# Gate and up columns of a feed-forward network by seven block products, in chunks of eight feature tiles

## The chip, the cores and the metric

One core of a Trainium2 chip. The metric is the device time of one execution in microseconds (us). The engines are TensorE (PE; its weight loads are listed apart as PEld), VectorE (DVE), ScalarE (ACT), GpSimd (POOL) and SyncE (SP), which issues most transfers. POOL can issue transfers too. Each engine executes its own instructions in order and waits on semaphores for the others.

## The reference

Two layers. Each adds a feed-forward network, a mixer and a second feed-forward network to x (512 tokens of 1024 features):

```python
def _rms_norm(x, g):
    y = xf * lax.rsqrt(jnp.mean(xf * xf, axis=-1, keepdims=True) + NORM_EPS)
    return y.astype(x.dtype) * g

def _swiglu(x, w_gate, w_up, w_down):
    return (jax.nn.silu(x @ w_gate) * (x @ w_up)) @ w_down

for l in range(DEPTH):
    x = x + 0.5 * _swiglu(_rms_norm(x, norm_ffn1[l]), ffn1_w_gate[l], ffn1_w_up[l], ffn1_w_down[l])
    h = _rms_norm(x, norm_mix[l])
    ...
    x = x + mix @ w_out[l]
    x = x + 0.5 * _swiglu(_rms_norm(x, norm_ffn2[l]), ffn2_w_gate[l], ffn2_w_up[l], ffn2_w_down[l])
```

The hidden size is 2816, so w_gate and w_up have 22 columns of 128 features, called features f below, and w_down has 8 columns of 128. All is float32. The mixer (three head groups: a recurrence, windowed attention and a convolution) isn't touched, apart from where one scratch buffer lies.

## The kernel before

x is held transposed: eight tiles x[j] of 128 features by 512 tokens. Every matrix is split into two parts that TensorE takes at its full pace: hi, the value cast to the reduced format F32R, and lo, the rest. A product of 128 x 128 weights with a tile is then three matmuls (`mm3`, L116): hi with the high part of x (L119), hi with its low part (L120), lo with the high part (L121). A weight block (`slot`, L105) is loaded by SP (L111) into one of three raw buffers, cast to hi by ACT (L112), and lo is a DVE subtract (L113); hi and lo have three buffers each.

A feed-forward network (`ffn`) first computes, for each f, the gate column and the up column. Each is 8 tiles x 3 matmuls of 512 tokens into one PSUM bank, 48 matmuls for an f. `gated` then multiplies gate (L216, DVE) and up (L218, DVE) by R, the norm's factor for each token, applies Silu (L217, ACT), multiplies both (L219, POOL), and splits the result into ah (L124, ACT) and al (L125, DVE), which stay in SBUF for all 22 features. Then each of the 8 down columns is one sum of 22 x 3 matmuls in PSUM, and L271 (DVE) adds half of it to x[j].

The norm is applied late: `norm_tile` gives xh (x times the norm's gain, cast, L172, ACT), xl (the rest, L173, DVE) and the square (L180, ACT), which POOL adds up (L181). The products run on xh and xl; the sum over features (L199, PE) and R follow while feature 0 and 1 are computed. At the mixer's end, x[j] gets its sum in L717 (DVE), and norm_tile(j) prepares the second network's input tile by tile. At the kernel's start the loads of the first two weight blocks stand among those of x.

The order of the work on each engine is set by a scheduler that looks at readiness, not by the order of the code alone. Tiles come from pools with a fixed number of buffers: a new tile waits for the last use of the one whose buffer it takes.

Of the kernel before, what the change touches and what calls it, by code (L numbers as in the profile page):

```python
# [21 lines left out]
EPS = 1e-6  # L22
RB = 3
# [15 lines left out]
HD = 64  # L39
NP = 3  # L40
# [41 lines left out]
class Kern:  # L82
# [71 lines left out]
    def tb(self, n):  # L154
        return self.tab[:, TAB[n][0] : TAB[n][1]]

    def norm_begin(self, idx):
        self.xp = self.tc.tile_pool(name=self.n("xp"), bufs=1, side="right")
        pool = self.xp.__enter__()
        xh = lambda j: pool.tile([P, T], F32R, tag=f"xh{j}", name=self.n("xh"))  # L160
        xl = lambda j: pool.tile([P, T], F32R, tag=f"xl{j}", name=self.n("xl"))
        self.xh, self.xl = [xh(j) for j in range(KT)], [xl(j) for j in range(KT)]
        pool.tile([P, XPAD], F32, name=self.n("xpad"))
        self.nidx = idx
        self.acc = self.nrm.tile([P, T], F32, tag="acc", name=self.n("acc"))

    def norm_tile(self, j):

        nc = self.nc
        x = self.x[j]  # L170
        g = self.gains[:, self.nidx * KT + j : self.nidx * KT + j + 1]
        nc.scalar.activation(self.xh[j], x, AF.Copy, scale=g)  # L172
        nc.vector.scalar_tensor_tensor(  # L173
            self.xl[j], x, g, self.xh[j].bitcast(F32), op0=ALU.mult, op1=ALU.subtract
        )
        if j == 0:
            nc.scalar.activation(self.acc, x, AF.Square)
        else:
            sq = self.nrm.tile([P, T], F32, tag=("sq", "R")[j % 2], name=self.n("sq"))
            nc.scalar.activation(sq, x, AF.Square)  # L180
            nc.gpsimd.tensor_tensor(self.acc, self.acc, sq, op=ALU.add)  # L181
# [31 lines left out]
    def gated(self, f, p, ap, tp, ah, al):
        nc = self.nc
        t = [tp.tile([P, T], F32, tag=q, name=self.n(q)) for q in ("g", "u", "s")]
        nc.vector.tensor_tensor(t[0], p[0], self.R, op=ALU.mult)  # L216
        nc.scalar.activation(t[2], t[0], AF.Silu)  # L217
        nc.vector.tensor_tensor(t[1], p[1], self.R, op=ALU.mult)  # L218
        nc.gpsimd.tensor_tensor(t[2], t[2], t[1], op=ALU.mult)  # L219
        ah.append(ap.tile([P, T], F32R, name=self.n("ah")))  # L220
        al.append(ap.tile([P, T], F32R, name=self.n("al")))
        self.split(ah[f], al[f], t[2])

    def ffn(self, l, n, nxt, last=False):
        nc, I = self.nc, self.I
        with self.tc.tile_pool(name=self.n("ffn"), bufs=1) as ap, self.tc.tile_pool(name=self.n("fft"), bufs=2) as tp:
            ah, al = [], []
            held = None
            for f in range(FT):
                p = []  # L230
                if f == 0 and l == 0 and n == 0:

                    both = [self.ahead.pop(0) for w in range(2)]
                    p = [self.psum() for w in range(2)]
                    for k in range(KT):
                        for (hi, lo), ps in zip(both, p):
                            s = slice(k * P, (k + 1) * P)
                            self.mm3(ps, hi[:, s], lo[:, s], self.xh[k], self.xl[k], k == 0, k == KT - 1)
                    self.norm_sum()
                    held = p  # L240
                    continue
                for w in range(2):
                    hi, lo = self.ahead.pop(0) if self.ahead else self.slot(I["wgu"][l, n, f, w], 1024)
                    ps = self.psum()
                    for k in range(KT):
                        s = slice(k * P, (k + 1) * P)
                        self.mm3(ps, hi[:, s], lo[:, s], self.xh[k], self.xl[k], k == 0, k == KT - 1)
                    p.append(ps)
                    if (f, w) == (0, 1):
                        self.norm_sum()  # L250
                    elif (f, w) == (1, 0):
                        self.norm_spread()
                if f == 0:
                    held = p
                    continue
                if held:
                    self.gated(f - 1, held, ap, tp, ah, al)
                    held = None
                self.gated(f, p, ap, tp, ah, al)
            self.norm_close()  # L260
            if nxt is not None:
                self.norm_begin(nxt)
            for j in range(KT):
                ps = self.psum()
                for q in range(0, FT, 8):
                    m = min(8, FT - q)
                    hi, lo = self.slot(I["wd"][l, n, j, :, q * P : (q + m) * P], m * P)
                    for k in range(m):
                        s = slice(k * P, (k + 1) * P)
                        self.mm3(ps, hi[:, s], lo[:, s], ah[q + k], al[q + k], q + k == 0, q + k == FT - 1)  # L270
                nc.vector.scalar_tensor_tensor(  # L271
                    self.x[j], ps, 0.5, self.x[j], op0=ALU.mult, op1=ALU.add
                )
                if nxt is not None:
                    self.norm_tile(j)
                    if nxt % 3 == 1:
                        nc.sync.dma_start(out=self.xs[:, j], in_=self.x[j])
                if last:
                    nc.sync.dma_start(out=self.out[:, j], in_=self.x[j])

    def feed(self, srcs):

# [7 lines left out]
    def mixer(self, l):  # L290
# [747 lines left out]
    def run(self):  # L1038
        nc, tc, I = self.nc, self.tc, self.I
        self.consts()  # L1040
        self.x = []
        for j in range(KT):
            if j in (0, 1):
                self.ahead.append(self.slot(I["wgu"][0, 0, 0, j], 1024))
            self.x.append(self.xt(j))
            nc.sync.dma_start(out=self.x[j], in_=I["xT"][:, j])
        self.xs = self.dp.tile([P, KT, T], F32, name="xs")
        self.norm_begin(0)
        for j in range(KT):
            self.norm_tile(j)  # L1050
        self.consts2()
        for l in range(self.depth):
            self.ffn(l, 0, 3 * l + 1)
            self.mixer(l)
# [24 lines left out]
def arrays(i):  # L1079
# [7 lines left out]
    A["wgu"] = c(gu.reshape(L, 2, 2, KT, P, FT, P).transpose(0, 1, 5, 2, 4, 3, 6).reshape(L, 2, FT, 2, P, KT * P))  # L1087
# [44 lines left out]
```

## Time and profile before

| | |
|---|---|
| median of 3 runs | 2079.12 us (2079.01 to 2082.44) |
| the profiled execution | 2079.0 us |
| its span, first to last instruction | 2077.2 us |
| ACT busy | 743.7 us (36%) |
| POOL busy | 335.5 us (16%) |
| read from HBM | 183.47 MB |

The span is shorter than the execution by 1.8 us, which lie around it. Busy times of PE are modelled at the end of a matmul, so what a matmul costs is read from the distance between starts. A group of instructions is a line with its engine, operation and tiles; its row gives the count, the busy time, the mean, and the idle time just before them with what ended it. A window's row gives for each engine the busy time in that stretch and the number of instructions, then the granted clock of TensorE as a share, the share of the transfer engines in use and GB/s.

### The profile page before, as it was taken

Reading aid. Unit: us, or ns where it says so; the run is one execution under the profiler, and the core shown is the slowest. Engines: PE = TensorE matmul, PEld = TensorE weight load, DVE = VectorE, ACT = ScalarE, POOL = GpSimd, SP = SyncE. Lnnn points to the kernel's source line nnn. Section 1 sums busy time; section 2 is a strip of 40 time slices with the busy share of each in tenths; the row PEclk is TensorE's granted clock in tenths of the full one; section 3 lists DMA queues with packets and bytes.
Section 4 is the critical chain, followed back from the end, with each engine's and each line's share of the span. In section 5 each row is a group of like instructions: output and inputs, shape, how many; then the busy total and the mean of one; then the engine's idle time right before and its main releaser. Section 6 shows DMA issues by size and latency. Waiting matters only on the chain. (4 is left out here: it accounts for less than half of the span.)

```text
span 2077.2 us, 26018 instructions
## 1 busy us (share of the span) xinstructions
PE 2033.1 (98%) x10406; PEld 1654.5 (80%) x10406; DVE 1122.4 (54%) x1565; ACT 743.7 (36%) x1136; POOL 335.5 (16%) x298
## 2 busy tenths in 40 slices
PE   8999999989999999999999999999899999999999
PEld 6888888768877788888888888887687677888887
DVE  5545433699766455543244554337997764454422
ACT  4332322454365332322232322325534653232221
POOL 3101101132411211110010111002323111110100
PEclk9999999999999999999999999999999999999999
DMA  4232333213212323233323232332133132333332
GB/s 169 92 102 93 95 109 124 80 57 92 78 42 89 109 92 99 94 97 100 98 91 102 92 101 89 120 112 90 44 92 90 33 105 92 94 100 102 99 109 66
DMA packets 81865, 193.80 MB, mean 93 GB/s; under 512 B 26640, under 2 KB 32272, under 8 KB 81744
## 3 DMA queue, kind: packets, MB, share of 16 engines
q1 hardware_dynamic: 81312, 191.79, 29.7%
q8 instruction: 81, 1.33, 0.3%
q10 hardware_dynamic: 432, 0.36, 0.1%
q14 instruction: 40, 0.33, 0.1%
HBM read 183.47 MB, written 8.65 MB: 92 GB/s over the span
## 5 line engine op out<-in xcount | busy, mean ns | idle before, releaser
L112 ACT CAST hi<-raw 128x1024 fp32r<-128x1024 f32 (+3 forms) x368 | 350.9, 954 | 991.0 <-PE psg L120 850.0
L113 DVE TENSOR_TENSOR lo<-raw,hi 128x1024 fp32r<-128x1024 f32 (+3 forms) x368 | 504.1, 1370 | 348.7 <-ACT hi L112 329.2
L119 PE MATMUL psg<-xh,hi 128*128 128x512 f32 x1632 | 642.9, 394 | 7.1 <-ACT xh L172 7.1
L120 PE MATMUL psg<-xl,hi 128*128 128x512 f32 x1632 | 641.1, 393 | 5.0 <-DVE xl L173 4.9
L121 PE MATMUL psg<-xh,lo 128*128 128x512 f32 x1632 | 641.0, 393 | 0.0
L120 PEld LDWEIGHTS psg<-xl,hi 128*128 128x128 f32 x1632 | 308.6, 189 | 74.3 <-DVE xl L173 8.9
L119 PEld LDWEIGHTS psg<-xh,hi 128*128 128x128 f32 x1632 | 308.6, 189 | 73.8 <-ACT xh L172 7.1
L121 PEld LDWEIGHTS psg<-xh,lo 128*128 128x128 f32 x1632 | 308.8, 189 | 66.4 <-issue 2.0
L119 PE MATMUL psg<-ah,hi 128*128 128x512 f32 x704 | 273.9, 389 | 0.0
L120 PE MATMUL psg<-al,hi 128*128 128x512 f32 x704 | 273.9, 389 | 0.0
L121 PE MATMUL psg<-ah,lo 128*128 128x512 f32 x704 | 273.9, 389 | 0.0
L219 POOL TENSOR_TENSOR s<-s,u 128x512 f32<-128x512 f32 x88 | 120.5, 1370 | 800.1 <-ACT hi L112 676.5
L218 DVE TENSOR_TENSOR u<-psg,R 128x512 f32<-128x512 f32 x88 | 60.8, 691 | 265.4 <-PE psg L121 265.1
L120 PEld LDWEIGHTS psg<-al,hi 128*128 128x128 f32 x704 | 132.2, 188 | 27.5
L121 PEld LDWEIGHTS psg<-ah,lo 128*128 128x128 f32 x704 | 132.2, 188 | 27.5
L119 PEld LDWEIGHTS psg<-ah,hi 128*128 128x128 f32 x704 | 132.2, 188 | 27.3
L216 DVE TENSOR_TENSOR g<-psg,R 128x512 f32<-128x512 f32 x88 | 60.8, 691 | 125.4 <-PE psg L121 125.4
L181 POOL TENSOR_TENSOR acc<-acc,sq 128x512 f32<-128x512 f32 x42 | 58.6, 1396 | 381.3 <-ACT sq L180 380.9
L1001 DVE SCALAR_TENSOR_TENSOR cacc<-z,par,cacc 128x482 f32<-128x482 f32 (+14 forms) x120 | 101.7, 847 | 1.7
L124 ACT CAST ah<-s 128x512 fp32r<-128x512 f32 x88 | 54.8, 623 | 121.7 <-POOL s L219 121.7
L125 DVE TENSOR_TENSOR al<-s,ah 128x512 fp32r<-128x512 f32 x88 | 59.8, 679 | 20.9 <-ACT ah L124 20.9
L867 PE MATMUL psg<-hi,xh 128*128 128x384 f32 x192 | 68.0, 357 | 1.3 <-ACT nat L892 1.3
(208 smaller groups left out, 1819.2 us busy)
## 6 DMA issues: line engine op xcount, KB each, us to landing
raw<-in_wgu_dram SPq DMA_DIRECT2D x176, 512.0 KB, 3.5
raw<-in_wd_dram SPq DMA_DIRECT2D x64, 512.0 KB, 3.5
raw<-in_win_dram SPq DMA_DIRECT2D x28, 512.0 KB, 3.5
raw<-in_wd_dram SPq DMA_DIRECT2D x32, 384.0 KB, 3.1
raw<-in_watt_dram SPq DMA_DIRECT2D x24, 384.0 KB, 3.0
raw<-in_wout_dram SPq DMA_DIRECT2D x28, 192.0 KB, 2.3
xs<-x SPq DMA_DIRECT2D x16, 256.0 KB, 2.0
x<-xs SPq DMA_DIRECT2D x16, 256.0 KB, 3.1
```

Of the source, the lines that this page charges most:

```text
L112: nc.scalar.copy(hi[:, :cols], raw[:, :cols])
L113: nc.vector.tensor_tensor(lo[:, :cols], raw[:, :cols], hi[:, :cols].bitcast(F32), op=ALU.subtract)
L119: mm(out, lhsT=whi, rhs=xhi, start=first, stop=False)
L120: mm(out, lhsT=whi, rhs=xlo, start=False, stop=False)
L121: mm(out, lhsT=wlo, rhs=xhi, start=False, stop=last)
L125: self.nc.vector.tensor_tensor(lo, src, hi.bitcast(F32), op=ALU.subtract)
L181: nc.gpsimd.tensor_tensor(self.acc, self.acc, sq, op=ALU.add)
L216: nc.vector.tensor_tensor(t[0], p[0], self.R, op=ALU.mult)
L218: nc.vector.tensor_tensor(t[1], p[1], self.R, op=ALU.mult)
L219: nc.gpsimd.tensor_tensor(t[2], t[2], t[1], op=ALU.mult)
L867: mm(o, lhsT=self.xh[kk][:, t], rhs=hi[:, s], start=kk == 0, stop=False)
L1001: nc.vector.scalar_tensor_tensor(a[:, d:], z[:, 0 : T - d], pa("dww", u * CW + j), a[:, d:], op0=ALU.mult, op1=ALU.add)
```

## The change

The tokens are cut into halves of 256, the eight x tiles into even and odd ones, and the gate and up columns are taken as the two halves of the output. That makes a 2 x 2 block product, which seven block products give instead of eight (Strassen's kind, with few additions). Each of the seven is 4 pairs of tiles x 3 matmuls of 256 tokens: 84 matmuls of 256 for an f, where there were 48 of 512.

For it the code adds:
- `norm_forms`: of every pair of x tiles seven forms (sums and differences of the halves), each split into fh (ACT) and fl (DVE). It takes the place of L172 and L173 for the two feed-forward networks; the mixer's norm keeps them.
- `forms`: the weights' seven forms of a feature. ba (two blocks) and s13 (two blocks) are loaded by SP; a transfer issued by POOL adds two further blocks onto s13 as it lands (L281). s24 is made by two DVE sums (L284, L285). dd, the seventh block, is loaded for two features at a time. The low parts of s13 and s24 are DVE subtracts (L269). Those of ba and dd are made by ACT writing -hi (L266) and a transfer issued by POOL that adds raw onto it (L267); in the first feature of the kernel they are subtracts too. s13 and s24 share three buffers, ba and dd the three raw ones.
- In `up`, one ACT copy and seven DVE adds of 256 (L334) put the four output blocks together; the scalings by R (L314, L316) then read SBUF.
- Chunks: after eight features (8, 8, 6) the eight down columns take them in, with a sum onto x each (L373), so there are three such rounds where there was one.
- The loads of the kernel's first weights are issued ahead of x's. The scratch of `norm_forms` for the second network lies in a buffer of the mixer.

The rows below are what DVE executes for one feature in the middle of the first network. Before (g and u are the scaled columns, lo a low part of weights, al of the result):

```order
L216 TENSOR_TENSOR g_688<-psg_632,R_279 128x512
L113 TENSOR_TENSOR lo_732<-raw_730,hi_731 128x1024
L218 TENSOR_TENSOR u_689<-psg_663,R_279 128x512
L113 TENSOR_TENSOR lo_774<-raw_772,hi_773 128x1024
L125 TENSOR_TENSOR al_696<-s_690,ah_695 128x512
```

And of the change, from the third add of one feature to its al:

```order
L334 TENSOR_TENSOR u_1863<-psb_1906,u_1863 128x256
L334 TENSOR_TENSOR u_1863<-psg_1878,u_1863 128x256
L269 TENSOR_TENSOR lo_1987<-s_314_1973,hi_1986 128x1024
L334 TENSOR_TENSOR g_1862<-psb_1921,g_1862 128x256
L334 TENSOR_TENSOR g_1862<-psg_1935,g_1862 128x256
L314 TENSOR_TENSOR g_1862<-g_1862,R_442 128x512
L284 TENSOR_TENSOR s_338_2113<-s_337_2110,ba_2108 128x512
L334 TENSOR_TENSOR u_1863<-psg_1949,u_1863 128x256
L269 TENSOR_TENSOR lo_1991<-s_316_1978,hi_1990 128x1024
L316 TENSOR_TENSOR u_1863<-u_1863,R_442 128x512
L285 TENSOR_TENSOR s_338_2113<-s_338_2113,ba_2108 128x512
L130 TENSOR_TENSOR al_1968<-g_1862,ah_1967 128x512
```

Two subtracts of 1024 are still there. Seven adds of L334 (two stand ahead of these rows) and the sums of the weights two features on (s_338 from s_337, which is an s13 with its second part already added) have come between them, ahead of al.

The second place is the start of the second feed-forward network of layer 0 on DVE. Before, from the sum onto the last x tile but one (psg of L717 is the mixer's output product):

```order
L717 TENSOR_TENSOR x_1049_5547<-psg_993_5350,x_1049_5547 128x512
L113 TENSOR_TENSOR lo_1064_5628<-raw_1062_5626,hi_1063_5627 128x1024
L717 TENSOR_TENSOR x_1054_5570<-psg_997_5372,x_1054_5570 128x512
L173 SCALAR_TENSOR_TENSOR xl_1016_5413<-x_1049_5547,gains_85,xh_1008_5405 128x512
L113 TENSOR_TENSOR lo_1069_5666<-raw_1067_5664,hi_1068_5665 128x1024
L173 SCALAR_TENSOR_TENSOR xl_1017_5414<-x_1054_5570,gains_85,xh_1009_5406 128x512
```

And of the change, from the sum onto the last tile (L848 is L717 of before; eo is the scratch, fl the low parts of forms):

```order
L848 TENSOR_TENSOR x_6995<-psg_6770,x_6995 128x512
L202 SCALAR_TENSOR_TENSOR fl_6803<-eo_6805,fh_6799 128x512
L192 TENSOR_TENSOR eo_6805<-eo_6805 128x256
L204 TENSOR_TENSOR fl_6803<-eo_6805,fh_6799 128x768
L194 SCALAR_TENSOR_TENSOR fl_6804<-eo_6805,fh_6800 128x256
L195 TENSOR_TENSOR fl_6804<-eo_6805,fh_6800 128x256
L198 TENSOR_TENSOR eo_6805<-eo_6805 128x256
L199 TENSOR_TENSOR eo_6805<-eo_6805 128x256
L200 TENSOR_TENSOR eo_6805<-eo_6805 128x256
L202 SCALAR_TENSOR_TENSOR fl_6804<-eo_6805,fh_6800 128x512
L227 TENSOR_SCALAR rnt<-psc_7179 128x4
L204 TENSOR_TENSOR fl_6804<-eo_6805,fh_6800 128x768
```

Where one low part of x stood behind the last sum, there are now the rest of two pairs of forms. Behind the last row come the two sums of s24 (L284, L285) and the two low parts (L269) of feature 0's weights. The load into that feature's s13 by SP waits for the form in the last row.

The third place is POOL in the same stretch as the first: transfers that add (DMA) and the products of `gated` (g times u) in one queue.

```order
L317 TENSOR_TENSOR g_1862<-g_1862,u_1863 128x512
L281 DMA s_357_2240<-in_wgu_dram 128x1024
L267 DMA lo_1995<-dd_1975 128x1024
L317 TENSOR_TENSOR g_1999<-g_1999,u_2000 128x512
L267 DMA lo_2115<-ba_2108 128x1024
L281 DMA s_380_2377<-in_wgu_dram 128x1024
```

Before, POOL had one product a feature here and no transfer; now two or three transfers are issued between two products.

The diff, cut to its core:

```diff
+    def norm_forms(self, j):
+        ...
+        if j % 2 == 0:
+            A.activation(e, x3, AF.Copy, scale=self.gains[:, g : g + 1])
+            A.activation(h[:, 0], e[:, 0], AF.Copy, scale=-1.0)
+            V.tensor_tensor(tf[:, 0], e[:, 1], e[:, 0], op=ALU.subtract)
+            A.copy(h[:, 3], tf[:, 0])
+            V.scalar_tensor_tensor(l[:, 0], e[:, 0], -1.0, f32(h[:, 0]), op0=ALU.mult, op1=ALU.subtract)
+            V.tensor_tensor(l[:, 3], tf[:, 0], f32(h[:, 3]), op=ALU.subtract)
+        else:
+            A.activation(o, x3, AF.Copy, scale=self.gains[:, g : g + 1])
+            V.tensor_tensor(tf[:, 1], o[:, 1], tf[:, 0], op=ALU.subtract)
+            V.tensor_tensor(tf[:, 2], e[:, 1], o[:, 1], op=ALU.subtract)
+            V.tensor_tensor(tf[:, 3], o[:, 0], tf[:, 1], op=ALU.subtract)
+            A.activation(h[:, 1:3], o, AF.Copy, scale=-1.0)
+            V.scalar_tensor_tensor(l[:, 1:3], o, -1.0, f32(h[:, 1:3]), op0=ALU.mult, op1=ALU.subtract)
+            A.copy(h[:, 4:7], tf[:, 1:4])
+            V.tensor_tensor(l[:, 4:7], tf[:, 1:4], f32(h[:, 4:7]), op=ALU.subtract)
+    def forms(self, l, n, f):
+        def parts(pool, tag, raw, dma):
+            ...
+            A.copy(hi, raw)
+            if dma:
+                A.activation(lo, hi.bitcast(F32), AF.Copy, scale=-1.0)
+                G.dma_start(out=lo, in_=raw, accum_op=ALU.add)
+            else:
+                V.tensor_tensor(lo, raw, hi.bitcast(F32), op=ALU.subtract)
+            return hi, lo
+        first = f == 0 and l == 0 and n == 0
+        ba = v(self.ring.tile([P, 1024], F32, tag="raw", name=self.n("ba")))
+        nc.sync.dma_start(out=ba, in_=v(w[l, n, f, :, 0 : 2 * k]))
+        s13 = self.ep.tile([P, 2, k], F32, tag="rs", name=self.n("s13"), bufs=ER)
+        nc.sync.dma_start(out=s13, in_=v(w[l, n, f, :, k : 3 * k]))
+        if f % 2 == 0:
+            dd = v(self.ring.tile([P, 1024], F32, tag="raw", name=self.n("dd")))
+            nc.sync.dma_start(out=dd, in_=w[l, n, f : f + 2, :, 3 * k : 4 * k].rearrange("f p k -> p f k"))
+        G.dma_start(out=s13, in_=v(w[l, n, f, :, 2 * k : 4 * k]), accum_op=ALU.add)
+        s24 = self.ep.tile([P, 2, k], F32, tag="rs", name=self.n("s24"), bufs=ER)
+        hba, lba = parts(self.ring, "i", ba, not first)
+        V.tensor_tensor(s24[:, 0], s13[:, 1], ba[:, 1], op=ALU.add)
+        V.tensor_tensor(s24[:, 1], s24[:, 0], ba[:, 0], op=ALU.add)
+        h13, l13 = parts(self.ep, "s", s13, False)
+        h24, l24 = parts(self.ep, "s", s24, False)
+        if f % 2 == 0:
+            self.hdd = parts(self.ring, "i", dd, not first)
+        ...
     def ffn(self, l, n, nxt, last=False):
+            def up(f, W, held):
+                def mul(i, r=range(KP)):
+                    ...
+                    for p in r:
+                        s = slice(p * P, (p + 1) * P)
+                        self.mm3(ps[i], hi[:, s], lo[:, s], self.fh[p][:, c], self.fl[p][:, c], p == 0, p == KP - 1)
+                add = lambda o, i, z: V.tensor_tensor(o, ps[i], z, op=ALU.add)
+                mul(1)
+                A.copy(g0, ps[1])
+                mul(5)
+                if f == 0:
+                    for i in (6, 7, 2, 3):
+                        mul(i, range(KP - 1))
+                    r = [KP - 1]
+                else:
+                    r = range(KP)
+                mul(6, r)
+                add(u1, 6, g0)
+                add(g1, 5, u1)
+                ...
+                mul(7, r)
+                add(u0, 7, u1)
+                add(u1, 5, u0)
+                mul(2, r)
+                add(g0, 2, g0)
+                mul(3, r)
+                add(g1, 3, g1)
+                mul(4)
+                add(u0, 4, u0)
+                ...
+            for q in range(0, FT, CH):
+                m = min(CH, FT - q)
+                items += [("up", f, q, m) for f in range(q, q + m)] + [("down", j, q, m) for j in range(KT)]
-        GG = [m1.tile([P, NC, 2, 2, HD], F32, name=self.n("GG")) for _ in range(NP)]
+        GG = [m1.tile([P, NC * 4 * HD], F32, tag=f"GG{q}", name=self.n("GG")).rearrange("p (c x h t) -> p c x h t", c=NC, x=2, h=2) for q in range(NP)]
-        self.norm_begin(3 * l + 2)
+        self.norm_begin(3 * l + 2, lambda: m1.tile([P, 8 * HT], F32, tag="GG0", name=self.n("eo")))
```

More of the change, by code (lines that the diff above doesn't have):

```diff
@@ L28 @@
 CPOS = 4
+HT = T // 2
+KP = KT // 2
+CH = 8
+ER = 3
+ES = 4
 CO = (1, 1)
@@ L165, in norm_begin @@
         self.acc = self.nrm.tile([P, T], F32, tag="acc", name=self.n("acc"))
+    def norm_forms(self, j):
+        nc = self.nc
+        V, A = nc.vector, nc.scalar
+        g = self.nidx * KT + j
+        e, o, tf = self.eo[:, 0], self.eo[:, 1], self.tf
+        h, l = self.fh[j // 2], self.fl[j // 2]
+        f32 = lambda a: a.bitcast(F32)
+        x3 = self.x[j].rearrange("p (t c) -> p t c", t=2)
+        if j % 2 == 0:
[14 more added lines that the diff above has]
+            V.tensor_tensor(l[:, 4:7], tf[:, 1:4], f32(h[:, 4:7]), op=ALU.subtract)
     def norm_tile(self, j):
@@ L170, in norm_tile @@
         x = self.x[j]
[L171 to L175, printed above, removed]
+        if self.nidx % 3 == 1:
+            g = self.gains[:, self.nidx * KT + j : self.nidx * KT + j + 1]
+            nc.scalar.activation(self.xh[j], x, AF.Copy, scale=g)
+            nc.vector.scalar_tensor_tensor(
+                self.xl[j], x, g, self.xh[j].bitcast(F32), op0=ALU.mult, op1=ALU.subtract
+            )
+        else:
+            self.norm_forms(j)
         if j == 0:
@@ L211, in norm_close @@
         self.xp.__exit__(None, None, None)
[L213 to L222, printed above, removed]
+    def forms(self, l, n, f):
+        nc, w = self.nc, self.I["wgu"]
+        V, A, G = nc.vector, nc.scalar, nc.gpsimd
+        k = KP * P
+        def parts(pool, tag, raw, dma):
+            hi = pool.tile([P, 2, k], F32R, tag="h" + tag, name=self.n("hi"), bufs=RB if tag == "i" else ES)
+            lo = pool.tile([P, 2, k], F32R, tag="lo" if tag == "i" else "ls", name=self.n("lo"), bufs=RB if tag == "i" else ES)
+            A.copy(hi, raw)
+            if dma:
+                A.activation(lo, hi.bitcast(F32), AF.Copy, scale=-1.0)
+                G.dma_start(out=lo, in_=raw, accum_op=ALU.add)
+            else:
+                V.tensor_tensor(lo, raw, hi.bitcast(F32), op=ALU.subtract)
+            return hi, lo
+        first = f == 0 and l == 0 and n == 0
+        v = lambda a: a.rearrange("p (x k) -> p x k", x=2)
+        ba = v(self.ring.tile([P, 1024], F32, tag="raw", name=self.n("ba")))
[14 more added lines that the diff above has]
+            self.hdd = parts(self.ring, "i", dd, not first)
+        hd, ld = self.hdd
+        return {
+            1: (hba[:, 1], lba[:, 1], 0),
+            2: (hba[:, 0], lba[:, 0], 1),
+            3: (h24[:, 1], l24[:, 1], 2),
+            4: (hd[:, f % 2], ld[:, f % 2], 6),
+            5: (h13[:, 1], l13[:, 1], 3),
+            6: (h24[:, 0], l24[:, 0], 4),
+            7: (h13[:, 0], l13[:, 0], 5),
+        }
@@ L224, in ffn, with down_slot @@
+    def down_slot(self, l, n, q, m, j):
+        return self.slot(self.I["wd"][l, n, j, :, q * P : (q + m) * P], m * P)
     def ffn(self, l, n, nxt, last=False):
         nc, I = self.nc, self.I
[L226 to L252, printed above, removed]
-                if f == 0:
-                    held = p
-                    continue
-                if held:
[L257 to L263, printed above, removed]
-                ps = self.psum()
[L265 to L273, printed above, removed]
@@ L279, in ffn, with prep @@
                     nc.sync.dma_start(out=self.out[:, j], in_=self.x[j])
+            items = []
+            for q in range(0, FT, CH):
+                m = min(CH, FT - q)
+                items += [("up", f, q, m) for f in range(q, q + m)] + [("down", j, q, m) for j in range(KT)]
+            def prep(i):
+                if i < len(items):
+                    kind, z, q, m = items[i]
+                    ready[i] = self.forms(l, n, z) if kind == "up" else self.down_slot(l, n, q, m, z)
+            ready, prev = {}, None
+            prep(0)
+            if self.late:
+                self.late()
+                self.late = None
+            for i, (kind, z, q, m) in enumerate(items):
+                prep(i + 1)
+                W = ready.pop(i)
+                if kind == "up":
+                    prev = up(z, W, prev)
+                    if z == 0:
+                        self.norm_sum()
+                else:
+                    if (z, q + m) == (0, FT):
+                        self.norm_close()
+                        if nxt is not None:
+                            self.norm_begin(nxt)
+                    down(z, q, m, W)
     def feed(self, srcs):
@@ L1041, in run, with late @@
         self.x = []
[L1042 to L1046, printed above, removed]
         self.xs = self.dp.tile([P, KT, T], F32, name="xs")
         self.norm_begin(0)
-        for j in range(KT):
-            self.norm_tile(j)
-        self.consts2()
+        def late():
+            for j in range(KT):
+                self.x.append(self.xt(j))
+                nc.sync.dma_start(out=self.x[j], in_=I["xT"][:, j])
+            for j in range(KT):
+                self.norm_tile(j)
+            self.consts2()
+        self.late = late
         for l in range(self.depth):
@@ L1086, in arrays @@
     gu = np.stack([np.stack([i[f"ffn{n}_w_gate"], i[f"ffn{n}_w_up"]], 1) for n in (1, 2)], 1)
[L1087 removed]
+    gu = gu.reshape(L, 2, 2, KP, 2, P, FT, P).transpose(0, 1, 6, 2, 4, 5, 3, 7).reshape(L, 2, FT, 4, P, KP * P)
+    A["wgu"] = c(gu[:, :, :, [1, 0, 2, 3]].transpose(0, 1, 2, 4, 3, 5).reshape(L, 2, FT, P, 4 * KP * P))
     wd = np.stack([i["ffn1_w_down"], i["ffn2_w_down"]], 1)
```

50 lines of the change are left out of this document (46 added, 4 removed).

## The prediction

> **What bounds the kernel now.** I read the page's shares first, then the chain that ended last, then stretches of the span, then single rows.
>
> ```profile
> PE 2033.1 (98%) x10406; PEld 1654.5 (80%) x10406; DVE 1122.4 (54%) x1565; ACT 743.7 (36%) x1136; POOL 335.5 (16%) x298
> core 0: 2077.2 us, clock 0.988
> PE psg L120 6%; PE psg L119 6%; PE psg L121 6%; PE psc L191 0%; PE psc L199 0%; DVE x L271 0%; DVE xl L173 0%
> 100.00:150.00 50.00, 50.00 (x222) 41.44 (x221) 26.17 (x24) 15.38 (x19) 6.46 (x5) 1.00 0.29 94
> 1030.00:1060.00 30.00, 30.00 (x139) 24.99 (x138) 7.59 (x8) 6.76 (x8) 4.81 (x3) 1.00 0.34 106
> ```
>
> TensorE has work 98% of the span, and the chain is matmuls. In a steady stretch of gate and up columns (100 to 150 us; the columns are PE, its weight loads, DVE, ACT, POOL, clock, DMA share, GB/s) PE is busy all 50 us, DVE about half; even the start of layer 1 (1030 to 1060) loses nothing. So fewer matmul columns shorten the time until something else is late; places where PE waits count in full.
>
> **The matmuls.** What one costs is read from starts, as their ends overlap:
>
> ```profile
> 199.73 0.39 PE L119 MATMUL psg<-xh,hi 128*128 128x512 f32 x1
> 209.93 0.39 PE L119 MATMUL psg<-xh,hi 128*128 128x512 f32 x1
> 504.83 0.33 PE L869 MATMUL psg<-hi,xl 128*128 128x384 f32 x1
> 511.94 0.34 PE L868 MATMUL psg<-lo,xh 128*128 128x384 f32 x1
> 590.94 1.19 PEld L1020 LDWEIGHTS psg<-onesm,z 128*128 128x128 f32 x10
> ```
>
> There are 45 steps from 199.73 to 209.93, so 226.7 ns for 512 columns; 41 from 504.83 to 511.94, so 173.4 ns for 384. That is 0.416 ns a column and 13 ns beside it, and 120 ns for 256 columns, a width that before doesn't have. Weight loads alone come every 0.11 us (ten in 1.19), just under it. The starts are given to 0.01 us, so the line is good to 1 ns: 119 is the lower bound. The upper is 125, a load of 112 and the 13 beside it with nothing overlapped. I take 120, on the line of the two rows. Before, 4 x 22 features x 48 = 4224 matmuls of 226.7 ns are 957.5 us; after, 88 x 84 = 7392 of 120.2 ns are 888.5. **Term 1: -69**, or 0.8 us a feature (10.88 to 10.08). Each ns on the 256-wide matmul is 7.4 us.
>
> **The up loop on DVE.**
>
> ```profile
> 699.85 1.23 DVE L113 TENSOR_TENSOR lo<-raw,hi 128x1024 fp32r<-128x1024 f32 x1 [5.17 <-ACT hi L112]
> 700.99 0.68 DVE L216 TENSOR_TENSOR g<-psg,R 128x512 f32<-128x512 f32 x1
> 701.59 0.68 DVE L218 TENSOR_TENSOR u<-psg,R 128x512 f32<-128x512 f32 x1
> 702.19 0.68 DVE L216 TENSOR_TENSOR g<-psg,R 128x512 f32<-128x512 f32 x1
> L113 DVE TENSOR_TENSOR lo<-raw,hi 128x256 fp32r<-128x256 f32 x12 | 5.1, 424 | 2.9 <-ACT hi L112 2.9
> 101.51 1.29 POOL L219 TENSOR_TENSOR s<-s,u 128x512 f32<-128x512 f32 x1 [9.59 <-ACT hi L112]
> 101.55 2.33 DVE L113 TENSOR_TENSOR lo<-raw,hi 128x1024 fp32r<-128x1024 f32 x1 [0.21 <-ACT hi L112]
> 106.99 1.23 DVE L113 TENSOR_TENSOR lo<-raw,hi 128x1024 fp32r<-128x1024 f32 x1 [0.21 <-ACT hi L112]
> L124 ACT CAST ah<-s 128x512 fp32r<-128x512 f32 x88 | 54.8, 623 | 121.7 <-POOL s L219 121.7
> ```
>
> Back to back, a 1024-wide subtract takes 1.14 us from start to start and a 512-wide operation 0.60; I give a 256-wide one 0.34 (0.424 less the same 0.08 of overlap). The new loop of a feature has seven adds of 256 (2.4), two low parts of 1024 (2.3), two sums of 512 (1.2), two scalings (1.2) and al (0.6): 7.7 us, against 4.1 now. The al at its end waits for the POOL product of the same feature (1.29) and ACT's ah (0.62); with the signals that is 2.3 us in which DVE, which executes in order, does only one sum of 512. The subtract at 101.55 beside a product took 2.33 instead of 1.23, so an operation on two SBUF tensors doesn't run beside the product. The loop is about 10.0 us, as long as PE's 10.08: nothing over, but not later by itself.
>
> Of this blocking the Trainium skill, "SBUF — State Buffer", section "SBUF: two separate sides", says that DVE with two SBUF inputs and GpSimd take turns on one pair of ports, whole instructions at a time; the two rows agree. [...]
>
> **Weight supply.** The s13 load of a feature waits for the low part of s24 two features back (three buffers). Then it lands, the accumulating transfer lands, and the sum on DVE can start.
>
> ```profile
> raw<-in_wgu_dram SPq DMA_DIRECT2D x176, 512.0 KB, 3.5
> raw<-in_wout_dram SPq DMA_DIRECT2D x28, 192.0 KB, 2.3
> 10.28 0.33 SPq L111 DMA_DIRECT2D raw<-in_wgu_dram  x1
> 8.00:14.00 6.00, 5.96 (x16) 3.92 (x17) 4.97 (x4) 5.34 (x9) 3.62 (x3) 1.00 1.05 407
> ```
>
> A 512 KB load lands in 3.5 us. No row has an accumulating transfer. It reads two streams, so I go by the slope of the two loads, 1.2 us per 320 KB, for 1 MB: 5.4 us. Bounds are 3.5 (a plain load) and 8 (two of them and queueing). With 0.4 for issue the supply takes L = 3.5 + 5.4 + 0.4 = 9.3 us, from 7 to 12. From a first sum to the low part of its s24 DVE has 10.3 us of work and 2.3 of waiting, so two features take L + 12.7: 11.0 each at 9.3, 0.9 over PE's. Five features of an eight-feature chunk are paced so (the others find weights loaded under the down products), three of six in the last; PE can live some 3 us on what PSUM and the buffers hold. 8 chunks x (5 x 0.9 - 3) = 12; the 4 small chunks lose nothing. **Term 2: +12**; from 0 at L = 8.7 or less, over +55 at 11, to +81 at 12. The volume speaks for the upper half: in 10.08 us 1.3 MB of plain loads and 1.3 MB accumulated, counted twice 3.9 MB or 390 GB/s, where the fullest stretch before has 407.
>
> By the Trainium skill, "DMA: Bandwidth & Descriptors", section "Anatomy of one DMA — SWDGE (gpsimd) path", a transfer from GpSimd's queue takes 2.0 us and its bytes at 436 GB/s, an estimate of 3.2 us for 512 KB; term 2 would be 0, the starts of term 4 some 2.2 each less, and the sum 2072.
>
> **The kernel's start.**
>
> ```profile
> 10.17 10.94 DVE L173 SCALAR_TENSOR_TENSOR xl<-x,gains,xh 128x512 fp32r<-128x512 f32 x7
> 10.22 12.04 POOL L181 TENSOR_TENSOR acc<-acc,sq 128x512 f32<-128x512 f32 x7 [8.54 <-ACT sq L180]
> 22.31 0.98 PEld L199 LDWEIGHTS psc<-ones,acc 128*128 128x128 f32 x8 [0.15 <-POOL acc L181]
> ```
>
> Before, seven low parts of x took 10.94 us for 4.8 us of work, as the squares' sums on POOL blocked them: 6 us. The first feature ended at 22.3. After, DVE has per pair of tiles six forms of 256, one of 512 and one of 768 (0.34, 0.68, 0.9): 3.6, so 14.5 for four pairs, and 5.8 for the first weights (four low parts, two sums); with the 6 of blocking 26.3. It begins near 9.5, since three weight loads now go ahead of x, and ends near 36; some 3 us of products follow. 39 against 22.3, and 0.8 that term 1 counted: **term 3: +17.5** (14 to 22).
>
> **Feature 0 of the second FFN, in each layer.**
>
> ```profile
> 679.55 0.68 DVE L717 TENSOR_TENSOR x<-psg,x 128x512 f32<-128x512 f32 x1
> 680.15 1.60 DVE L173 SCALAR_TENSOR_TENSOR xl<-x,gains,xh 128x512 fp32r<-128x512 f32 x1
> 680.00:685.00 5.00, 2.66 (x11) 1.60 (x10) 4.68 (x4) 1.24 (x2) 2.50 (x2) 0.98 0.33 105
> 685.00:690.00 5.00, 5.00 (x16) 3.93 (x16) 1.23 (x1) 1.04 (x1) 0.00 (x0) 0.68 0.54 151
> 692.14 1.08 PEld L199 LDWEIGHTS psc<-ones,acc 128*128 128x128 f32 x8
> 1715.00:1720.00 5.00, 4.22 (x12) 3.40 (x13) 1.96 (x3) 1.04 (x1) 0.00 (x0) 0.66 0.31 109
> ```
>
> The last sum of x starts at 679.55, PE waits 2.3 us, its clock falls to 0.68 for some 5 us, and feature 0 ends at 692.1. After, DVE still has behind that sum the rest of two pairs of forms (5.2 us of work, 2 for ACT's casts between them, 2.5 of blocking): about 690. The first s13's load there waits for that last form, since its buffer lies over the form's scratch; L = 9.3 gives 699, two sums and a low part 701. From the high part (700) PE has six products, 8.7 us, and 1.7 for the low clock: 710.4, and with the 0.8 of term 1 **+19 each; term 4: +39** with 0.5 for the queue behind SP's wait. Bounds are 12 (forms run without ACT waits or blocking, L = 7) and 23 (L = 12). PE idles longer here than now, so a lower clock for longer is in the upper bound.
>
> **Smaller.** The start of layer 1 has no such wait for its s13, but twice the forms: **+4** (0 to 8). Twelve changes from up to down products instead of four: behind the last product stand an add, a low part, a scaling, POOL's product, ah and al (0.34 + 1.14 + 0.6 + 1.29 + 0.62 + 0.68, and 0.4 of signals), 5.1 us; a down product of eight features needs that al after 22 matmuls of 226.7 ns, 5.0 us, one of six after 16, 3.6. 4 x 1.5 = **+6** (0 to 15). The 64 further sums of x on DVE (0.69 each) lie beside down products: 24 matmuls are 5.4 us in which DVE has one sum and one low part; nothing. The rest of the mixer keeps its instructions: nothing.
>
> Sum: -69 + 12 + 17.5 + 39 + 4 + 6 = +9.5. The profiled execution took 2079.0 (span 2077.2 and 1.8 around it), and the median before is 2079.1: **2088.5**.
>
> **The rivals.**
> *Everything new is hidden (faster).* L = 7 takes term 2 away (-12) and 2.3 from each start of term 4; if ACT and POOL don't interrupt the forms, 4.5 more each, and the kernel's start is +14: 2088.5 - 12 - 4.6 - 9 - 3.5 = 2059.4. For it: DVE idles 46% now, and loads have a share of 0.29. Against: the 10.94 us at the start, and 679.55 to 692.1.
> *The up loop is bound by supply (slower).* If each accumulating transfer waits behind a DVE operation, about 1.2 us, L = 10.5 and two features take 23.2: 1.5 over each, 8 x (7.5 - 3) + 4 x (4.5 - 3) = 42 in place of 12, 2118.5; at L = 11, 2131.5. It decides from L = 8.7. The same would follow from PSUM adds slower than 0.34: 0.1 more is 0.7 a loop.
> *The 256-wide matmul is bound by its weight load.* At 125 ns +37, 2125.5; against it the 0.11 us loads.
> That the products aren't saved can't be: PE's rows after have 84 of 256 columns for each feature.
>
> **How the numbers follow.** Forecast 0.42 (alone 2070 to 2105), hidden 0.27, supply 0.23, weight load 0.08. The low end is the first rival without the transitions and layer 1's 4 us (2049), taken as 2047; L = 12 with term 4's bound gives 2088.5 + 69 + 8 = 2165, and up to 2140 leaves about 1 in 10 above. The measurement tells 0.2% (4.2 us) from no change: below 2075 lie the first rival and a fifth of the forecast's 0.42, 0.36; within, 0.12 of the forecast's; above, the rest, 0.52.
>
> **What would show it.** Starts 0.120 us apart in the up stretches; PE busy all of such a stretch if term 2 is 0, else gaps from the third feature of a chunk on with DVE's sum waiting for an s13 transfer; s13's landing times against 3.5 and 5.4; the first feature's end near 39 us, and the second FFN's some 30 us after its last x sum. Wrong if PE's gaps lie inside down products or the mixer, or if the 256-wide pace is off by over 3 ns.

## The result and the profile after

The changed kernel is slower: 2399.38 us (median of 4 runs, 2397.99 to 2401.59) against 2079.24, a ratio of 1.1537 with a 95% interval of 1.1517 to 1.1557. The prediction was 2088.5 with a range up to 2140. The sign was right, the size was not. The profiled execution has a span of 2396.1 us, 318.9 more than before.

The page after: shares of the engines, the transfer queues (packets, MB, share of the 16 transfer engines' time), the chain that ended last, and the transfers with their KB and median time from issue to landing.

```profile
PE 2081.7 (87%) x13574; PEld 1835.5 (77%) x13574; DVE 1454.0 (61%) x2519; ACT 1051.8 (44%) x1550; POOL 544.8 (23%) x516
q1 hardware_dynamic: 93280, 214.86, 27.3%
q0 software_dynamic: 31392, 114.31, 26.0%
DMA 7%; PE 4%; DVE 3%; issue 2%; POOL 1%; ACT 1%; POOLq 0%; SPq 0%; DVEq 0%; ACTq 0%
ba<-in_wgu_dram SPq DMA_DIRECT2D x88, 512.0 KB, 5.0
s<-in_wgu_dram SPq DMA_DIRECT2D x88, 512.0 KB, 4.7
s<-in_wgu_dram POOLq DMA_DIRECT2D x88, 512.0 KB, 6.6
lo<-ba POOLq DMA_DIRECT2D x87, 512.0 KB, 6.9
```

PE fell from 98% to 87% of a longer span. The chain could be followed back over 18% of the span only; in that part transfers have the largest share. The queue that before didn't have, q0, holds the adding transfers. It moved about half as many bytes as q1 in nearly the same engine time. An adding transfer of 512 KB lands in 6.6 to 6.9 us in the median, and the plain loads beside it have gone from 3.5 to 4.7 and 5.0.

Where the time went is read from the sums onto x (DVE), which end each stage. As an example, the first network of layer 1, with its start and end in each kernel:

```profile
1042.60 0.69 DVE L271 SCALAR_TENSOR_TENSOR x<-psg,x 128x512 f32<-128x512 f32 x1 [1.95 <-PE psg L121]
1403.52 0.69 DVE L271 SCALAR_TENSOR_TENSOR x<-psg,x 128x512 f32<-128x512 f32 x1 [1.95 <-PE psg L121]
```

```profile
1224.88 0.68 DVE L373 SCALAR_TENSOR_TENSOR x<-psg,x 128x512 f32<-128x512 f32 x1
1641.41 0.69 DVE L373 SCALAR_TENSOR_TENSOR x<-psg,x 128x512 f32<-128x512 f32 x1 [1.33 <-PE psg L126]
```

The first two rows are before's, 360.9 us; the other two after's, 416.5. All six stages, worked out in the same way (e4 is an experiment below, the change without any adding transfer):

| stage, us | before | after | e4 |
|---|---|---|---|
| layer 0, first network (with the kernel's start) | 372.6 | 460.8 | 376.1 |
| layer 0, mixer | 306.9 | 315.8 | 309.4 |
| layer 0, second network | 363.0 | 448.3 | 362.2 |
| layer 1, first network | 360.9 | 416.5 | 346.0 |
| layer 1, mixer | 306.9 | 309.4 | 312.4 |
| layer 1, second network | 363.1 | 441.5 | 358.2 |

The first network of layer 1 has no costly start, so its 55.6 us are taken as what the steady part of every network lost: 4 x 55.6 = 222 of the 319. The rest, 97, belongs to the kernel's start (460.8 - 416.5, less the 11.7 that before shows there: 32.6) and to the second networks with the mixers' ends ahead of them (38.6 and 25.3).

Inside a network the loss is in the up stretches. From the last down product of one chunk to the first of the next chunk (less its 24 matmuls of 226.7 ns, 5.4 us) lie eight features. After, and e4:

```profile
195.78 0.68 DVE L373 SCALAR_TENSOR_TENSOR x<-psg,x 128x512 f32<-128x512 f32 x1
308.05 0.69 DVE L373 SCALAR_TENSOR_TENSOR x<-psg,x 128x512 f32<-128x512 f32 x1 [0.82 <-PE psg L126]
```

```profile
157.07 0.69 DVE L371 SCALAR_TENSOR_TENSOR x<-psg,x 128x512 f32<-128x512 f32 x1 [3.42 <-PE psg L126]
243.61 0.69 DVE L371 SCALAR_TENSOR_TENSOR x<-psg,x 128x512 f32<-128x512 f32 x1 [0.82 <-PE psg L126]
```

That is 106.8 / 8 = 13.35 us a feature after, and 81.1 / 8 = 10.14 in e4, where 84 matmuls of 120 ns are 10.08. Before, a feature took 10.88. What PE does meanwhile is shown by a window over each of the two stretches, first after, then e4:

```profile
192.00:302.00 110.00, 89.60 (x673) 87.18 (x673) 59.67 (x105) 45.14 (x57) 24.20 (x23) 0.92 0.69 168
160.00:240.00 80.00, 80.00 (x659) 79.57 (x658) 59.89 (x105) 45.74 (x56) 9.73 (x8) 1.00 0.33 109
```

In the changed kernel PE is idle for 20.4 of the 110 us, some 2.5 us a feature, and the granted clock is 0.92 where e4 has 1.00. Most of what is left of the 3.2 us goes with that clock: behind a wait of 3.65 us, shown below, the matmuls start 0.21 us apart from 236 to 241 us, where the granted clock is 0.50, and then 0.12 again. From 200 to 302 us 68 of 604 matmuls start 0.20 to 0.23 us apart, which is an estimated 0.8 us a feature.

What stands between two features is seen in rows of the timelines of DVE, SP and POOL of the changed kernel, put in order of time (start, duration, engine, line; in brackets the idle time before and what ended it):

```profile
213.98 1.22 DVE L269 TENSOR_TENSOR lo<-s,hi 128x1024 fp32r<-128x1024 f32 x1
215.22 0.33 SPq L277 DMA_DIRECT2D s<-in_wgu_dram  x1
219.81 0.88 POOL L281 DMA_DIRECT2D s<-in_wgu_dram  x1 [2.26 <-DMA s<-in_wgu_dram]
224.94 0.69 DVE L284 TENSOR_TENSOR s<-s,ba 128x512 f32<-128x512 f32 x1 [2.63 <-issue]
226.48 1.22 DVE L269 TENSOR_TENSOR lo<-s,hi 128x1024 fp32r<-128x1024 f32 x1
227.72 0.33 SPq L277 DMA_DIRECT2D s<-in_wgu_dram  x1
```

The low part of one s24 ends at 215.2 and its buffer is free. The next s13 load goes out at once, and POOL's wait for it ends at 219.8; the adding transfer follows and has landed 5.0 us after its issue, at 224.9. DVE, idle for 2.63 us until then (the row itself names no cause), makes the sum, and **close behind it** the low part of the next s24 (that of the feature ahead of the one just summed), whose end lets the next load go at 227.7. So this chain closes once a feature: 12.5 us here.

A second chain stands beside it:

```profile
235.96 0.58 PE L126 MATMUL psg<-fh,lo 128*128 128x256 f32 x1 [3.65 <-DMA lo<-ba]
235.97 0.33 SPq L275 DMA_DIRECT2D ba<-in_wgu_dram  x1
243.45 0.69 DVE L284 TENSOR_TENSOR s<-s,ba 128x512 f32<-128x512 f32 x1 [7.92 <-DMA ba<-in_wgu_dram]
```

At 235.96 a low part's adding transfer has landed. PE had waited 3.65 us for it, and in the same moment SP can issue the next ba, since that transfer was the last reader of a raw buffer. DVE then idles 7.92 us for this ba. SP issues in order, so what stands behind such a load waits with it. Over the whole span the second chain weighs more on DVE's sum than the first: of the 451 us that DVE idles before L284, 310 end with a ba load.

```profile
L284 DVE TENSOR_TENSOR s<-s,ba 128x512 f32<-128x512 f32 x88 | 60.9, 692 | 451.4 <-DMA ba<-in_wgu_dram 310.3
```

### The profile page after: what moved, and what is told of

It reads as the page before. It is cut to its first block, busy times and chain, and to the rows that moved or that the text cites. A ratio compares the mean times of both kernels' runs of the same rounds, so it can differ in the third digit from the quotient of the medians.

```text
span 2396.1 us, 34389 instructions
## 1 busy us (share of the span) xinstructions
PE 2081.7 (87%) x13574; PEld 1835.5 (77%) x13574; DVE 1454.0 (61%) x2519; ACT 1051.8 (44%) x1550; POOL 544.8 (23%) x516
## 3 DMA queue, kind: packets, MB, share of 16 engines
q1 hardware_dynamic: 93280, 214.86, 27.3%
q0 software_dynamic: 31392, 114.31, 26.0%
## 5 line engine op out<-in xcount | busy, mean ns | idle before, releaser
L126 PE MATMUL psg<-fh,lo 128*128 128x256 f32 x1760 | 538.8, 306 | 134.2 <-DMA lo<-ba 125.2
L124 PE MATMUL psg<-fh,hi 128*128 128x256 f32 x1760 | 540.1, 307 | 117.8 <-DVE u L334 61.5
L125 PE MATMUL psg<-fl,hi 128*128 128x256 f32 x1760 | 531.4, 302 | 3.6 <-DVE fl L194 1.3
L126 PEld LDWEIGHTS psg<-fh,lo 128*128 128x128 f32 x1760 | 373.0, 212 | 145.6 <-DMA lo<-ba 135.1
L124 PEld LDWEIGHTS psg<-fh,hi 128*128 128x128 f32 x1760 | 372.4, 212 | 132.7 <-DVE u L334 68.9
L125 PEld LDWEIGHTS psg<-fl,hi 128*128 128x128 f32 x1760 | 372.3, 212 | 5.3 <-DVE fl L194 1.9
L284 DVE TENSOR_TENSOR s<-s,ba 128x512 f32<-128x512 f32 x88 | 60.9, 692 | 451.4 <-DMA ba<-in_wgu_dram 310.3
L269 DVE TENSOR_TENSOR lo<-s,hi 128x1024 fp32r<-128x1024 f32 x176 | 218.6, 1243 | 41.3 <-ACT hi L264 40.7
L118 DVE TENSOR_TENSOR lo<-raw,hi 128x1024 fp32r<-128x1024 f32 (+3 forms) x192 | 197.4, 1028 | 39.9 <-ACT hi L117 29.5
L125 PE MATMUL psb<-fl,hi 128*128 128x256 f32 x704 | 201.9, 287 | 1.3 <-DVE fl L202 1.3
L124 PE MATMUL psb<-fh,hi 128*128 128x256 f32 x704 | 201.2, 286 | 0.0
L281 POOL DMA_DIRECT2D s<-in_wgu_dram x88 | 78.6, 894 | 416.2 <-DMA s<-in_wgu_dram 324.7
```

The lines of the kernel that those rows point to most:

```text
L118: nc.vector.tensor_tensor(lo[:, :cols], raw[:, :cols], hi[:, :cols].bitcast(F32), op=ALU.subtract)
L124: mm(out, lhsT=whi, rhs=xhi, start=first, stop=False)
L125: mm(out, lhsT=whi, rhs=xlo, start=False, stop=False)
L126: mm(out, lhsT=wlo, rhs=xhi, start=False, stop=last)
L269: V.tensor_tensor(lo, raw, hi.bitcast(F32), op=ALU.subtract)
L281: G.dma_start(out=s13, in_=v(w[l, n, f, :, 2 * k : 4 * k]), accum_op=ALU.add)
```

## The experiments

Each ran once. Before, run beside them on the same chips, took 2082.5 us (e1 to e4), 2079.0 (e5 to e8) and 2086.7 (e9 to e12), so nothing is read from a difference of 8 us or less. e2 to e5 and e9 to e11 leave sums out, and their results lack these; the others make all of them. The expectations go by these theories. S and Q: short buffers make chains through transfers (S the s13 chain alone, Q both). R: the raw buffers alone. B: the transfers' work fills the 16 engines. e5 adds W: only the waits and their order count.

| run | us | a feature in the second up stretch |
|---|---|---|
| after | 2399.4 | 13.35 |
| e1 four buffers for s13 and s24 | 2377.5 | 12.53 |
| e2 nothing added onto s13 | 2215.6 | 11.44 |
| e3 nothing added for the low parts | 2187.5 | 11.53 |
| e4 no adding transfer | 2069.8 | 10.14 |
| e5 same transfers, plain | 2220.7 | 11.66 |
| e6 low parts added from HBM | 2360.7 | 12.97 |
| e7 e6 with five buffers | 2314.8 | 12.21 |
| e8 all sums on DVE | 2187.9 | 11.15 |
| e9 e3 with five buffers | 2146.3 | 10.40 |
| e10 e2 with the low parts from HBM | 2145.3 | 11.04 |
| e11 e7 with plain transfers | 2144.5 | 10.80 |
| e12 low parts on DVE, five buffers | 2168.2 | 10.87 |

The last column is one of four like stretches, one in each network; in the same run these differ by up to 0.9 us (after: 12.81 to 13.72).

**One buffer more (e1).** ER is the number of buffers that s13 and s24 share.

```diff
-ER = 3
+ER = 4
```

> One more buffer for s13 and s24 (4 instead of 3); result unchanged. Theory S (supply loop): the s13 load waits for the low part of s24, which on DVE stands behind the sum that waits for the s13 ahead of it, so one feature takes the load (4.7), the adding transfer (6.6) and some 2.4 us, 13.7 in all. With a fourth buffer the load waits for the low part of an s13 instead, earlier by more than a feature's work: up features fall to 11 to 12 us and the time to 2160 to 2230. Theory R (raw ring): ba's load waits until the adding transfer of an earlier low part has read its raw buffer, and SP's other loads queue behind it: no change, 2370 to 2400. Theory B (transfers in all): the 16 engines are short of room, 2340 to 2390.

22 us less, so S by itself is out. The raw chain, which was there before, is left. SP's waits of ba's load for a low part's adding transfer (in all, how many, the longest), first in after, then in e1:

```profile
SPq L275 <- DMA lo<-ba: 372.7, 46, 32.2
SPq L275 <- DMA lo<-ba: 412.3, 59, 11.6
```

The time lies in R's range and in B's. e2 and e3, next, take R alone out too, and e2 lies 34 us below B's range.

**Parts left out (e2, e3, e4).**

```diff
-        G.dma_start(out=s13, in_=v(w[l, n, f, :, 2 * k : 4 * k]), accum_op=ALU.add)
```

```diff
-                G.dma_start(out=lo, in_=raw, accum_op=ALU.add)
```

e2 leaves out the first, e3 the second, e4 both.

> The transfer that adds the second two blocks onto s13 is left out, so s13, s24 and all that follows lack these blocks; every other instruction stays. S: the loop is the load, 4.7 and 2.4, under PE's 10.1: some 2090 to 2120. R: the raw buffers are held as before: 2280 to 2350. B: one of 2.5 adding transfers a feature is gone, 40% of the loss: 2250 to 2290.

> The transfers that add raw onto -hi for the low parts of ba and dd are left out, so these low parts are -hi; every other instruction stays. S: s13's adding transfer has the engines to itself and lands in 4.5 to 5.5: up features of 11 to 12 us, 2160 to 2230. R: the whole loss of the up stretches goes: 2090 to 2120. B: 60% of it: 2190 to 2230.

> Both kinds are left out (s13 lacks two blocks, the low parts of ba and dd are -hi). All three theories: up features at 10.1 to 10.5 us, so what is left over 2079 - 69 are the starts, the transitions and DVE: 2060 to 2110.

Without any of them the kernel takes 2069.8 us and its up stretches are PE's; so 330 us of the 2399 hang on the adding transfers, and matmuls, forms, DVE's adds and chunks together gain 13 against the run of before beside it. Neither kind alone explains it: leaving out either gives back 184 or 212 us, and 1.3 and 1.4 us a feature more than in e4 stay. Leaving one out takes away its chain and its work, so these runs don't yet tell chains from work; the next six are for that.

**Adding or only transferring (e5), and the chains opened (e6, e7).**

```diff
-                G.dma_start(out=lo, in_=raw, accum_op=ALU.add)
+                G.dma_start(out=lo, in_=raw)
-        G.dma_start(out=s13, in_=v(w[l, n, f, :, 2 * k : 4 * k]), accum_op=ALU.add)
+        G.dma_start(out=s13, in_=v(w[l, n, f, :, 2 * k : 4 * k]))
```

> The same transfers from POOL's queue with the same waits, but without the addition: they overwrite, so s13 is its last two blocks and the low parts of ba and dd are raw. Theory Q (two chains through short buffers: s13's load and addition between two low parts of s24; ba's raw buffer held until its low part has been added, with SP's loads queued behind): each is as long as its transfers take to land; if a plain one lands in 3.5 to 4.5 us instead of 6.6, up features take 10.8 to 11.5 us and the time is 2130 to 2200. Theory B (the adding transfers fill the engines; about twice a plain one's work for a byte): their work falls from some 10 to some 7 us a feature: 2070 to 2120. Theory W (only the waits and their order count, not what a transfer costs): 2350 to 2400.

```diff
-                G.dma_start(out=lo, in_=raw, accum_op=ALU.add)
+                G.dma_start(out=lo, in_=src, accum_op=ALU.add)
```

Here src is the weights in HBM. e7 has ER = 5 besides.

> The low parts of ba and dd get raw added from HBM instead of from the raw buffer, which is then free as soon as ACT has cast it; result unchanged. Q: the raw chain is open, s13's stays at the landing times of after: 2300 to 2380. B: no change or slower by more HBM reads, 2380 to 2420.

> Low parts added from HBM and five buffers for s13 and s24, so both chains are open; result unchanged. Q: up features at 10.3 to 11.2 us, 2100 to 2190. B: the transfers' own work of 10 to 10.5 us a feature at the share of 0.84 that e1 reached gives 12.5: 2350 to 2400.

The queue row and the landing rows of e5:

```profile
q0 software_dynamic: 31392, 114.31, 15.2%
s<-in_wgu_dram POOLq DMA_DIRECT2D x88, 512.0 KB, 4.3
lo<-ba POOLq DMA_DIRECT2D x87, 512.0 KB, 4.4
```

The same bytes in the same packets, not adding, took 15.2% of e5's span of 2218.9, 337 us; adding, 26.0% of 2396.1, 623 us. **Adding costs 1.85 times the engine time of a plain transfer**, and landing goes from 4.3 to 6.6. That the engines are fuller in after isn't the reason: the packets of q1 took 654 us there (27.3%) and 668 in e5 (30.1% of its span). The change from adding to plain is 179 us of the time (2399.4 to 2220.7). But plain transfers with the same waits are still 151 above e4, so transfers and waits cost without any adding, too. W falls; Q and B each had a share of it right (Q's 2130 to 2200 missed 2220.7 by little, B's 2120 by 100).

e6's 2360.7 lies in Q's range, 39 us below after. e7, with both chains open, took 2314.8, outside Q's range and B's: the chains alone are not the loss. The window of e7's second up stretch:

```profile
193.00:290.00 97.00, 81.62 (x625) 80.05 (x624) 61.33 (x105) 44.67 (x55) 24.71 (x24) 0.91 0.74 172
```

The transfer engines are busy 74% of it (before, 29% in such a stretch), and PE loses 15 us of 97.

**One chain opened at a time, and both with plain transfers (e9, e10, e11).** e9 is e3 with ER = 5; e10 is e2 with e6's edit; e11 is e7 with e5's.

> As e3 (no transfers that add raw onto -hi, these low parts stay -hi), with five buffers for s13 and s24. Theory Q: e3's 11.5 us a feature were s13's chain alone; open, up features are PE's 10.1 to 10.3 and the time e4's, 2068 to 2085. Theory B: the transfers' work is unchanged from e3, 2170 to 2190.

> As e2 (nothing added onto s13), with raw for the low parts added from HBM, so the raw buffers come free at ACT's cast. Q: e2's 11.4 us were the raw buffers' chain alone; 2068 to 2100. B: 2200 to 2230, as e2 or a little more.

> As e5 (all transfers, none adding), with the low parts' transfer from HBM and five buffers for s13 and s24, so both chains are open and the transfers' work is some 8 us a feature: Q: 2068 to 2100. B, if some 0.6 to 0.85 of the engines is all that can be used: 2130 to 2230. Together with e7 it tells whether what is left in e7 (2315) is the adding.

The window of e9's second up stretch:

```profile
175.00:255.00 80.00, 78.98 (x652) 78.15 (x651) 58.60 (x101) 42.94 (x54) 14.40 (x13) 1.00 0.57 145
```

With the s13 chain open, PE works 99% of it and a feature takes 10.40 instead of e3's 11.53: the chain was what held e3 in the up stretches. The time, 2146.3, still misses Q's 2085 (and B's 2170): only 28 of its 76 us over e4 are in four steady networks (353.0 against 346.0 in layer 1), the others are at the starts, where an adding transfer stands in series; that this makes all of them was not tried. In e10 opening the raw chain gives 0.4 us a feature here and 0.8 to 1.2 in the other networks, and PE's largest wait is directly for a low part's transfer, 55 us; its 2145.3 lies between the ranges of Q and B. In e11 both chains are open and nothing adds: 10.80, and e5's 2220.7 becomes 2144.5, in B's range and not in Q's. e7 and e11 differ only in the adding: **170 us** (178 when each is taken against the run of before beside it). Whether that is the room on the transfer engines or the further waits that a landing of 7.3 to 8.3 us instead of 4.7 to 5.3 makes (POOL's queue in order, the three buffers of the low parts) was not tried apart and stays open.

After, e5, e7 and e11 make a table of two by two, which splits the 330 us that lie between after and e4. Adding costs 179 us with both chains closed and 170 with them open. Opening the chains gives 85 us where transfers add and 76 where they don't. The last 75 us, from e11 to e4, stay with the plain transfers even so. One thing besides differs between the two pairs: in e7 and e11 the low parts' transfers read HBM, in after and e5 the raw buffers.

**Sums on the engines (e8, e12).** In both every sum is made.

```diff
-            if dma:
+            if False:
-        G.dma_start(out=s13, in_=v(w[l, n, f, :, 2 * k : 4 * k]), accum_op=ALU.add)
+        nc.sync.dma_start(out=s24, in_=v(w[l, n, f, :, 2 * k : 4 * k]))
+        V.tensor_tensor(s13, s13, s24, op=ALU.add)
```

e12 has the first edit with ER = 5, e8 both with ER = 6.

> No adding transfer, result unchanged: s13's second part is loaded plainly into the buffer of s24 and summed by DVE, and all low parts are DVE subtracts (ACT still writes -hi first); six buffers for s13 and s24. DVE gets 2.85 us a feature more, 10.5 of work and 2.3 of waits on the product and ah: 12.8 us a feature if nothing hides the waits, 2300; 10.6 if the scheduler fills them, 2115. Theories Q and B both take the transfers out of it; it tells how much DVE can carry.

> Result unchanged: s13 by the adding transfer, all low parts by DVE, five buffers for s13 and s24; no raw buffer waits for an adding transfer and one adding transfer is left a feature. Q: DVE decides as in e8 (11.15 us a feature) less its sum of s13 (1.14): 10.1 to 10.6, 2080 to 2130. B: 2170 to 2230.

They are 211 and 231 us faster than the change, and 109 and 82 slower than the run of before beside each. e8 lies between its two forecasts, 2115 and 2300 (with the edit ACT's -hi is gone, too); e12 lies between Q's range and B's. e8's chain is PE 43%, DVE 35%, transfers 3%: the transfers no longer set the pace. That it is DVE which keeps a feature at 11.15 us is read from this chain and was not tried. In layer 1's first network, which has no start to pay, they take 372.0 and 366.6, still over before's 360.9. So no version with all its sums made was found that beats before.

## Why the prediction was wrong, point by point

**Bound now and term 1 (right).** The 256-wide matmul takes 120 ns. The first and the last row of a PE timeline of e4 (102 rows, 101 steps):

```profile
199.82 0.28 PE L125 MATMUL psg<-fl,hi 128*128 128x256 f32 x1
211.94 0.28 PE L124 MATMUL psb<-fh,hi 128*128 128x256 f32 x1
```

The rival of the weight load falls with it. DVE's loop was sized rightly as well, in e4's rows: adds of 256 follow each other at 0.34 us, al waits 1.8 us for ah, and e4's up stretches are bound by PE.

**Term 2, the weight supply (the step that failed).** The text said "two features take L + 12.7", 11.0 us each; 13.35 were measured. It followed the data from a sum to the low part of the same s24, a feature later, and left out that DVE executes in order: the sum for the next feature's s24 stands *ahead* of that low part, as the order rows of DVE in the section on the change show (L284, then L269 two rows on). So a feature, not two, takes L and some 2.4 us. With L = 9.3 that is 11.7 instead of 11.0; with the measured 4.7 + 6.6 + 0.3 = 11.6 it is 14.0, where 13.35 is the mean of a stretch whose first features are loaded ahead. The bounds of L, 7 to 12, did hold its value; at 11.6 the formula gives +72, where the steady parts of after and e4 differ by 282 (70.5 in layer 1's first network, four times). That 14.0 comes near 13.35 doesn't make this chain the whole cause, as e1 shows.

**A chain that wasn't seen.** That ba's raw buffer is held until the adding transfer has read it was in no term. Yet 310 of the 451 us that DVE idled before its sum ended with a ba load. Opening the first chain alone gave 22 us (e1), the second alone 39 (e6), both 85 (e7).

**The price of adding (mis-sized).** 5.4 us was taken, from a plain transfer's slope for twice the bytes; it was 6.6. The plain loads beside it became 1.2 to 1.5 slower, but 0.9 to 1.3 of that is there in e5 too, where nothing adds (4.4 and 4.8). "Counted twice" was near the 1.85 that e5 shows, yet the sum drew only a wait from it, where adding by itself costs 170 to 179 us.

**Terms 3 and 4, the starts (mechanism right, size right only without adding).** For e4, worked out as above for after: the kernel's start +18.4 (predicted 17.5), the second networks with the mixers' ends +16.6 and +15.5 (predicted 19.5). In the changed kernel 32.6, 38.6 and 25.3: +96.5 where 56.5 was predicted. The series of load, adding transfer and cast at a moment when nothing is loaded ahead can be read in layer 0's second network: from the issue of the s13 load (785.74) to the landing of the adding transfer 12.6 us, where L was taken as 9.3 and 12 at most, 8.2 of them the adding transfer; PE waits 10.8 us for the cast behind it. How much of the 40 us is this series was not tried. That the rest of the mixer costs nothing was wrong by some 2.5 to 9 us: the forms stand on DVE among the low parts of the output weights.

**Smaller terms.** The start of layer 1 and the transitions: predicted +5.5 for the first network of layer 1 (4 and 1.5). In e4 this network gained 14.9 where term 1 alone gives 17.3, so they were 2.4. Without term 2 the whole sum is 2076.5; e4, which has no adding transfer, took 2069.8.

**The sign (luck in part).** The forecast of +9.5 stands on term 2's +12; without it the sum is 2.5 below before, and e4 took 13 us less than the run of before beside it. The sign came out right because the supply cost far more than was worked out for it.

**The rivals.** The supply rival named the right place, but its price and the point from which it decides, L = 8.7, came from the same formula; with a feature for each L + 2.4 that point is 7.7. Its condition, that an adding transfer waits behind a DVE operation for some 1.2 us, no run shows: in after the adding transfers that POOL issued while DVE was busy for over 80% of the issue (135 of 218) took 0.87 us to issue and landed in 6.5, those with DVE busy for under 20% of it (60) 0.86 and 6.6 (medians). By the fit of the Trainium skill for a transfer from GpSimd's queue ("DMA: Bandwidth & Descriptors", section "Anatomy of one DMA — SWDGE (gpsimd) path") 512 KB take an estimated 3.2 us. The fastest plain transfer onto s13 in e5 is near it, 3.4; the adding ones in after took 4.4 at the least, 5.0 onto s13.

## What to carry to other kernels

A transfer that adds isn't free arithmetic: ask what it costs per byte, and who can't go on until it has landed. When a sum is moved to a transfer, draw every chain that runs from a freed buffer over load, addition and the next use back to the buffer, through the engines' program order and not only through the data, and compare its length for one step with the work of that step. A saving of 7% on the bound engine is only there if the supply chain of each step stays below it.

## What the runs showed of the hardware

Not expected were three things. An adding transfer from POOL takes 1.85 times the transfer engines' time of a plain one with the same packets (623 against 337 us for 114.31 MB), and its issue holds POOL longer, by the rows of its line in the two kernels (durations in ns, least, median, most):

```profile
L281 POOL DMA_DIRECT2D s<-in_wgu_dram x88: 856/873/1237, 7.5 to 2318.9; - x88
```

```profile
L281 POOL DMA_DIRECT2D s<-in_wgu_dram x88: 530/539/717, 7.4 to 2144.9; - x88
```

The first is after, the second e5. And in the kernel's start two sums of squares on POOL took 7.72 us together, the first of them 6.4, where the median of all 42 is 1.4, while DVE ran operations on SBUF tensors without a gap; PE waited 5.29 us for the result:

```profile
34.30 7.72 POOL L223 TENSOR_TENSOR acc<-acc,sq 128x512 f32<-128x512 f32 x2 [4.86 <-ACT sq L222]
44.20 1.87 PE L241 MATMUL psc<-ones,acc 128*128 128x1 f32 x8 [5.29 <-POOL acc L223]
```

By these rows a dense run on DVE held POOL for several of DVE's instructions, not one. This was read from the trace and not tried by itself.
